# Weight splits behind a norm's vector steps, the mean square and the attention weights on ScalarE

## The chip, the cores and the metric

The kernel runs on one core of a Trainium2 chip. The metric is the device time of one execution in microseconds (us); three runs of the kernel before give 1181.78, 1181.87 and 1183.03, with a median of 1181.87. The engines are called PE (TensorE matmul; PEld is its weight load), ACT (ScalarE), DVE (VectorE), POOL (GpSimd) and SP (SyncE, which only issues DMAs here).

## The reference

Two layers of one block and one of another follow each other on 256 tokens of width 1024, all in fp32:

```python
for l in range(2):                                   # first block, twice
    z = rms_norm(x, g_pre_mix[l]) @ w_in[l]
    q, k, v, cb, cc, cx, ga, gb = split(z)           # 16 heads, 4 kv heads of 64
    y_attn = band_attention(rope(q), rope(k), v, sink) @ w_attn_proj[l]
    y_conv = (cb * short_conv(cc * cx, conv_w[l])) @ w_conv_proj[l]
    mix = (sigmoid(ga) * y_attn + sigmoid(gb) * y_conv) @ w_out[l]
    x = x + rms_norm(mix, g_post_mix[l])
    h = rms_norm(x, g_pre_ffn[l])
    f = (silu(h @ w_gate[l]) * (h @ w_up[l])) @ w_down[l]
    x = x + rms_norm(f, g_post_ffn[l])
mod = silu(c) @ w_cond_2 + b_cond_2                  # second block, once
# shift, scale and gate for each half come from mod; stick-breaking attention and
# a pooling mixer, w_out_2, then the same FFN shape, each with pre and post norm
```

rms_norm multiplies a row by (mean of its squares + 1e-6) to the power -1/2 and by a gain; the attention's p is exp(s - m), divided by the sum of its row plus exp(sink - m).

## The kernel before

The two halves of the tokens are t=0 and t=1, each 128 rows with its x in a tile of 128x1024. All weights are packed on the host into 211 chunks of 128x2048 (1 MB), which are consumed in one order, ORDER. To keep fp32 accuracy on PE every weight and every activation is split into a high part H (a cast to fp32r on ACT, L271) and a low part L (the difference, a DVE subtract, L272), and each product is three matmuls: high by H, low by H, high by L. A chunk is split in two halves of 128x1024; there are nine half buffers for H and nine for L (NSPLIT). get() hands out the next chunk: it issues raw loads on SP's queue up to five chunks ahead (LOOK_RAW, four raw buffers) and splits up to three chunks ahead (LOOK). Chunks of the kind "cond" are used raw, by DVE, and their sum over partitions is made on POOL (L504).

A scheduler sets the order within each engine from its own model of priorities and readiness; hp() gives the vector steps of a norm a higher priority. The names in the rows: mix_out does the wo products (tiles wo), ffn does gate, up and down (pgA/puA, pg/pu, dn; f is the gated product and fHL its two parts). At the end of wo and of dn the last chunks are held (three for wo, TAIL = 4 for dn) and used first for t=0 and then for t=1, so that the norm of t=0 runs while PE works on t=1. That norm is: Post.half (Square of the product with its sum, jk_a..., on ACT, L337; times the gain on DVE, ag, L397), Post.fin (rstd on POOL, L341, L343, L345; x update on DVE, L404, for both halves of the columns), Norm.vec (Square of x, jk_x..., L337; times the gain, xg, L362; rstd; the scale, L366, or L368 where a shift is added), and then Norm.tr: PE transposes (pt, L377) and the copies to the parts of the next input (xf, xm; ACT L207 and DVE L208). There are five such places: after wo and after dn of layer 0, after wo and after dn of layer 1, and after the second block's wo.

The attention of a layer is eight units, one for each of four kv heads and each t, interleaved with the matmuls of the convolution branch (pcc, pcx, pcb). In a unit: qs (split of q), pq (transposes), S (scores), mask and maximum on DVE, exp on ACT (L636, four of 128x256), the sink's exp es, den and its reciprocal rd on DVE (L641), P times rd, four POOL instructions (L643), eight PE transposes PTp (L651), their copies PT on ACT, and po.

Of the kernel before, what the change touches and what calls it, by code (L numbers as in the profile page):

```python
# [10 lines left out]
F32 = mybir.dt.float32  # L11
F32R = mybir.dt.float32r
# [6 lines left out]
P = 128  # L19
# [9 lines left out]
NDOWN = DFF // 256  # L29
TAIL = 4  # L30
EPS = 1e-6
# [127 lines left out]
def tile_model(ctx: ExitStack, tc: tile.TileContext, x_in, wpack, sink, convw, gains, c_in,  # L159
# [84 lines left out]

    state = dict(raw=0, spl=0, use=0)
    raws, HL = {}, {}
# [10 lines left out]

    def emit_split():
        i = state["spl"]
        while state["raw"] <= i:  # L260
            emit_raw()
        if ORDER[i][0] == "cond":
            HL[i] = raws[i]
        else:
            r = raws[i]
            hv = []
            for hf in range(2):
                H = wp.tile([P, CH // 2], F32R, tag="H", name=f"H{i}_{hf}", bufs=NSPLIT)
                L = wp.tile([P, CH // 2], F32R, tag="L", name=f"L{i}_{hf}", bufs=NSPLIT)
                rv = r[:, hf * (CH // 2):(hf + 1) * (CH // 2)]  # L270
                nc.scalar.copy(H, rv)  # L271
                nc.vector.tensor_sub(L, rv, H.bitcast(F32))  # L272
                hv.append((H, L))
            HL[i] = hv
        state["spl"] += 1

    def get(key):
        i = state["use"]
        assert ORDER[i] == key, (ORDER[i], key)
        n = len(ORDER)  # L280
        while state["raw"] < min(i + LOOK_RAW, n):
            emit_raw()
        while state["spl"] < min(i + LOOK, n):
            emit_split()
        state["use"] += 1
        return HL.pop(i)
# [20 lines left out]
    nhalf = cst.tile([P, 1], F32, tag="nhalf", name="nhalf")  # L307
    nc.vector.memset(nhalf, -0.5)
    ident_r = cst.tile([P, P], F32R, tag="identr", name="ident_r")
    nc.vector.tensor_copy(ident_r, ident)  # L310
# [23 lines left out]

    def sumsq(src, c, ssq, name):
        junk = s2(f"jk_{name}{c}")
        nc.scalar.activation(junk, src, AF.Square, accum_out=ssq[:, c:c + 1])  # L337

    def rstd(ssq, name):
        ms = small("ms_" + name, 1)  # L340
        nc.gpsimd.tensor_scalar(ms, ssq[:, 0:1], 1.0 / D, EPS, ALU.mult, ALU.add)  # L341
        m2 = small("m2_" + name, 1)
        nc.gpsimd.tensor_scalar(m2, ssq[:, 1:2], 1.0 / D, ms[:, 0:1], ALU.mult, ALU.add)  # L343
        rs = small("rs_" + name, 1)
        nc.gpsimd.tensor_tensor(rs, m2, nhalf, ALU.pow)  # L345
        return rs

    class Norm:
# [6 lines left out]
        def vec(self):  # L355
            t, name = self.t, self.name
            with hp():
                ssq = small("sx_" + name, 2)
                xg = s4("xg_" + name)
                for c in range(2):  # L360
                    sumsq(xt[t][:, HC[c]], c, ssq, "x" + name)
                    nc.vector.tensor_mul(xg[:, HC[c]], xt[t][:, HC[c]], self.G[:, HC[c]])  # L362
                rs = rstd(ssq, "x" + name)
                for c in range(2):
                    if self.S is None:
                        nc.vector.tensor_scalar(xg[:, HC[c]], xg[:, HC[c]], rs[:, 0:1], None, ALU.mult)  # L366
                    else:
                        nc.vector.scalar_tensor_tensor(xg[:, HC[c]], xg[:, HC[c]], rs[:, 0:1], self.S[:, HC[c]],  # L368
                                                       ALU.mult, ALU.add)
            self.h = xg  # L370
# [101 lines left out]
    def mix_out(l, kts, mp, make_post, after, lead):  # L472
        accs = [[ps1(f"wo{l}_{t}{c}") for c in range(2)] for t in range(2)]
        for i, j in enumerate(kts[:lead]):
            w = get(("wo", l, j))
            tick()
            for t in range(2):
                for c in range(2):
                    mmD2(accs[t], w, mp.ks(0, 2 * j, 2), mp.ks(1, 2 * j, 2), t, c, i == 0, False)
        drain()  # L480
        ch = [(get(("wo", l, j)), mp.ks(0, 2 * j, 2), mp.ks(1, 2 * j, 2)) for j in kts[lead:]]
        row_out(ch, accs, lead > 0, make_post, after)
# [24 lines left out]
    def ffn(l, xp, norms, make_post, after):  # L507
# [28 lines left out]
        for key in order:  # L536
# [13 lines left out]
            else:  # L550
# [9 lines left out]
                else:  # L560
                    tail.append((get(key), fs[j][0], fs[j][1]))
        if l == DEPTH - 1:
# [5 lines left out]
    def attention(l, q, kf, v, op):  # L568
# [35 lines left out]
        def unit(g, t):  # L604
# [37 lines left out]
            for hh in range(4):  # L642
                nc.gpsimd.tensor_scalar(Pt[:, hh, :], Pt[:, hh, :], rd[:, hh:hh + 1], 0.0, ALU.mult, ALU.add)  # L643
            yield SM_DELAY
# [232 lines left out]
    for l in range(DEPTH):  # L877
# [72 lines left out]
    def after3(t, post):  # L950
        post.fin()
        norms[t].vec()
        spawn(norms[t].gen, TR_DELAY)

# [5 lines left out]
    drain()  # L960
    aw = [(get(("wo", 2, j)), mp.ks(0, 2 * j, 2), mp.ks(1, 2 * j, 2)) for j in (0, 1)]
    for t in range(2):
# [74 lines left out]
```

## Time and profile before

| | |
|---|---|
| runs, median | 1181.87 us (1181.78 to 1183.03) |
| profiled execution | 1181.56 us, span 1179.7 us |
| granted PE clock, mean | 0.948 |
| busy PE / PEld / DVE / ACT / POOL | 97% / 81% / 71% / 56% / 11% of the span |
| HBM read | 233.28 MB |

The span is from the first to the last instruction; the execution's own time has 1.9 us more. A row of the timeline gives start, duration, engine, line, operation, output<-inputs, and in brackets how long the engine had been idle and what released it. The wait list gives engine, instruction, what it waited for, then the total in us, the number and the longest. Rows of groups give busy us and the mean in ns; those of windows give for each engine busy us, then the granted clock, the DMA share and GB/s.

### The profile page before, as it was taken

To read this page: it belongs to the slowest core of one execution; us is meant where nothing else is said; L and a number is where in the kernel's file an instruction comes from. 1 tells how busy PE (TensorE), PEld (TensorE's weight loads), DVE (VectorE), ACT (ScalarE), POOL (GpSimd) and SP (SyncE) were. 2 spreads that over 40 slices of the span, in tenths; PEclk is the share of its full clock that TensorE was granted. 3 is DMA by queue.
4 is the path that set the end of the run, shared out by engine and by line. 5 is a ranking of instruction groups with operands and counts; after the bars stand their busy time and mean duration, and the time that the engine had idled before them with its cause. 6 is when DMAs were issued, how large, how long until landed. Compare 5 with 4: busy or idle time off the path is not lost.

```text
span 1179.7 us, 15598 instructions
## 1 busy us (share of the span) xinstructions
PE 1145.0 (97%) x5896; PEld 957.7 (81%) x5896; DVE 837.0 (71%) x1146; ACT 659.6 (56%) x1107; POOL 126.5 (11%) x146
## 2 busy tenths in 40 slices
PE   6999999999999999999999999999999999999997
PEld 4887888878888887887888878888887777888886
DVE  6787845769788757787757768887968448765652
ACT  5775756556555446676646455555455546655451
POOL 0011310010202001013230012020212002000000
PEclk9998999999999999999999999999999999999999
DMA  8742334756666665634447556675865345655520
GB/s 316 281 143 108 136 140 171 268 183 251 240 257 248 223 241 188 241 107 143 144 168 296 198 181 232 233 297 187 314 255 196 127 161 179 245 178 184 201 85 36
DMA packets 36243, 235.36 MB, mean 200 GB/s; under 512 B 4668, under 2 KB 5180, under 8 KB 9416
## 3 DMA queue, kind: packets, MB, share of 16 engines
q1 hardware_dynamic: 33696, 225.41, 52.7%
q10 hardware_dynamic: 2472, 8.96, 2.3%
q8 instruction: 46, 0.75, 0.3%
q14 instruction: 29, 0.24, 0.1%
HBM read 233.28 MB, written 1.07 MB: 199 GB/s over the span
## 4 chain that ended last, share of the span: by engine, by line
PE 49%; DVE 3%; POOL 2%; ACT 2%; issue 1%; POOLq 0%; DVEq 0%; ACTq 0%
PE dn L242 9%; PE pu L242 9%; PE pg L242 8%; PE wo L242 2%; PE pcp L242 2%; PE pap L242 2%; PE pgb L242 2%; PE pga L242 2%; PE puA L242 1%; PE pgA L242 1%; PE pcx L242 1%; PE z L242 1%; PE pv L242 1%; PE p2k L242 1%; PE po L242 1%
## 5 line engine op out<-in xcount | busy, mean ns | idle before, releaser
L272 DVE TENSOR_TENSOR L<-raw,H 128x1024 fp32r<-128x1024 f32 x374 | 476.7, 1284 | 178.2 <-ACT H L271 168.4
L271 ACT CAST H<-raw 128x1024 fp32r<-128x1024 f32 x374 | 390.5, 1050 | 210.3 <-issue 33.8
L242 PE MATMUL dn<-H,fHL 128*128 128x512 f32 x432 | 116.4, 391 | 0.4 <-DVE fHL L548 0.2
L242 PE MATMUL pu<-xf,H 128*128 128x512 f32 x432 | 108.2, 392 | 0.0
L242 PE MATMUL pg<-xf,H 128*128 128x512 f32 x432 | 107.8, 391 | 0.0
L242 PEld LDWEIGHTS dn<-H,fHL 128*128 128x128 f32 x432 | 79.8, 188 | 16.7 <-ACT fHL L547 0.6
L242 PEld LDWEIGHTS pg<-xf,H 128*128 128x128 f32 x432 | 79.2, 188 | 15.2
L242 PEld LDWEIGHTS pu<-xf,H 128*128 128x128 f32 x432 | 77.7, 189 | 13.9
L643 POOL TENSOR_SCALAR P<-P,rd 128x256 f32<-128x256 f32 x64 | 46.9, 750 | 228.2 <-ACT cc L428 107.6
L242 PE MATMUL dn<-L,fHL 128*128 128x512 f32 x216 | 67.1, 390 | 0.0
L242 PEld LDWEIGHTS pg<-xf,L 128*128 128x128 f32 x432 | 58.9, 190 | 4.2
L242 PEld LDWEIGHTS pu<-xf,L 128*128 128x128 f32 x432 | 58.9, 190 | 4.2
L504 POOL PARTITION_ALL_REDUCE mrow<-cacc x6 | 38.9, 6486 | 217.4 <-DMA raw<-in_wpack_dram 177.4
L501 DVE SCALAR_TENSOR_TENSOR cacc<-raw,silu_c,cacc 128x1024 f32<-128x1024 f32 x48 | 61.3, 1277 | 0.2
L242 PE MATMUL pu<-xf,L 128*128 128x256 f32 x432 | 60.2, 282 | 0.0
L242 PE MATMUL pg<-xf,L 128*128 128x256 f32 x432 | 60.2, 282 | 0.0
L242 PE MATMUL wo<-H,m 128*128 128x512 f32 x192 | 52.5, 394 | 0.0
L547 ACT CAST fHL<-f 128x512 fp32r<-128x512 f32 x27 | 16.7, 620 | 57.3 <-DVE f L545 57.3
L242 PEld LDWEIGHTS dn<-L,fHL 128*128 128x128 f32 x216 | 40.6, 188 | 8.5
L242 PEld LDWEIGHTS wo<-H,m 128*128 128x128 f32 x192 | 35.6, 188 | 7.2 <-issue 0.2
L636 ACT ACTIVATE P<-S,nm 128x256 f32<-128x256 f32 x64 | 29.4, 473 | 12.2 <-DVE nm L630 12.2
L541 ACT ACTIVATE s<-s 128x512 f32<-128x512 f32 x27 | 17.1, 632 | 33.1 <-DVE s L429 33.1
(277 smaller groups left out, 2006.4 us busy)
## 6 DMA issues: line engine op xcount, KB each, us to landing
raw<-in_wpack_dram SPq DMA_DIRECT2D x209, 1024.0 KB, 4.9
raw<-in_wpack_dram SPq DMA_DIRECT2D x4, 512.0 KB, 8.8
gpm<-in_gains_dram ACTq DMA_DIRECT2D x3, 512.0 KB, 7.4
gpf<-in_gains_dram ACTq DMA_DIRECT2D x3, 512.0 KB, 8.0
gqf<-in_gains_dram ACTq DMA_DIRECT2D x2, 512.0 KB
out_dram<-x SPq DMA_DIRECT2D x4, 256.0 KB, 2.1
pmat<-in_pmat_dram SPq DMA_DIRECT2D x2, 384.0 KB, 5.5
x<-in_x_dram SPq DMA_DIRECT2D x2, 256.0 KB, 2.6
```

Of the source, the lines that this page charges most:

```text
L242: nc.tensor.matmul(o, a, b, start=start, stop=stop, **kw)
L271: nc.scalar.copy(H, rv)
L272: nc.vector.tensor_sub(L, rv, H.bitcast(F32))
L501: nc.vector.scalar_tensor_tensor(a3, w[:, k], silu_c[:, 2 * j + k:2 * j + k + 1], a3, ALU.mult, ALU.add)
L504: nc.gpsimd.partition_all_reduce(mrow, a, P, bass_isa.ReduceOp.add)
L541: last = nc.scalar.activation(s, s, AF.Silu)
L547: nc.scalar.copy(fHL[:, 0], fv)
L636: nc.scalar.activation(Pt[:, hh, :], S[hh // 2][:, hh % 2, :], AF.Exp, bias=nm[:, hh:hh + 1], accum_out=den[:, hh:hh + 1])
L643: nc.gpsimd.tensor_scalar(Pt[:, hh, :], Pt[:, hh, :], rd[:, hh:hh + 1], 0.0, ALU.mult, ALU.add)
```

## The change

Four things are edited.

- The splits are emitted by halves, and from the end of the first such norm on each split is issued behind the last ACT step (its Identity) and the last DVE step (its scale) of the last t=0 norm. Where chunks are held, no more than nine halves are handed out ahead (cap). TAIL goes from 4 to 3.
- The mean square: the Square has a scale of D to the power -1/2, so that its sum is the mean; an ACT Identity on 128x1 adds eps and, for the second half, the first half's sum. Two POOL steps (L341, L343) go; the power stays on POOL.
- P times rd is an ACT copy with a scale for each partition instead of a POOL instruction: 64 in all.
- A constant tile for eps.

POOL has 112 instructions fewer (64 and 48), ACT 112 more; PE has the same ones.

```diff
--- before.py
+++ after.py
@@ -27,7 +27,7 @@
 DFF = 2816
 NFB = (DFF - 512) // 256
 NDOWN = DFF // 256
-TAIL = 4
+TAIL = 3
 EPS = 1e-6
 NEG = -1e30
 CH = 2048
@@ -242,7 +242,7 @@
         nc.tensor.matmul(o, a, b, start=start, stop=stop, **kw)
 
 
-    state = dict(raw=0, spl=0, use=0)
+    state = dict(raw=0, spl=0, use=0, behind=None)
     raws, HL = {}, {}
 
     def emit_raw():
@@ -255,33 +255,39 @@
         raws[i] = t
         state["raw"] += 1
 
-    def emit_split():
-        i = state["spl"]
+    def behind(e):
+
+        return tc.issue_after(state["behind"][e].ins) if state["behind"] else nullcontext()
+
+    def emit_half():
+        i, hf = divmod(state["spl"], 2)
         while state["raw"] <= i:
             emit_raw()
         if ORDER[i][0] == "cond":
             HL[i] = raws[i]
         else:
-            r = raws[i]
-            hv = []
-            for hf in range(2):
-                H = wp.tile([P, CH // 2], F32R, tag="H", name=f"H{i}_{hf}", bufs=NSPLIT)
-                L = wp.tile([P, CH // 2], F32R, tag="L", name=f"L{i}_{hf}", bufs=NSPLIT)
-                rv = r[:, hf * (CH // 2):(hf + 1) * (CH // 2)]
+            H = wp.tile([P, CH // 2], F32R, tag="H", name=f"H{i}_{hf}", bufs=NSPLIT)
+            L = wp.tile([P, CH // 2], F32R, tag="L", name=f"L{i}_{hf}", bufs=NSPLIT)
+            rv = raws[i][:, hf * (CH // 2):(hf + 1) * (CH // 2)]
+            with behind(0):
                 nc.scalar.copy(H, rv)
+            with behind(1):
                 nc.vector.tensor_sub(L, rv, H.bitcast(F32))
-                hv.append((H, L))
-            HL[i] = hv
+            HL.setdefault(i, []).append((H, L))
         state["spl"] += 1
 
-    def get(key):
+    def get(key, cap=None):
+
         i = state["use"]
         assert ORDER[i] == key, (ORDER[i], key)
         n = len(ORDER)
         while state["raw"] < min(i + LOOK_RAW, n):
             emit_raw()
-        while state["spl"] < min(i + LOOK, n):
-            emit_split()
+        ahead = min(i + LOOK, n) * 2
+        if cap is not None:
+            ahead = max(min(ahead, cap), 2 * i + 2)
+        while state["spl"] < ahead:
+            emit_half()
         state["use"] += 1
         return HL.pop(i)
 
@@ -306,6 +312,8 @@
     nc.sync.dma_start(xt[1], x_in[P:2 * P, :])
     nhalf = cst.tile([P, 1], F32, tag="nhalf", name="nhalf")
     nc.vector.memset(nhalf, -0.5)
+    eps = cst.tile([P, 1], F32, tag="eps", name="eps")
+    nc.vector.memset(eps, EPS)
     ident_r = cst.tile([P, P], F32R, tag="identr", name="ident_r")
     nc.vector.tensor_copy(ident_r, ident)
     modd = dr.tile([6, D], F32, tag="modd", name="modd")
@@ -333,16 +341,15 @@
 
 
     def sumsq(src, c, ssq, name):
+
         junk = s2(f"jk_{name}{c}")
-        nc.scalar.activation(junk, src, AF.Square, accum_out=ssq[:, c:c + 1])
+        nc.scalar.activation(junk, src, AF.Square, scale=D ** -0.5, accum_out=ssq[:, c:c + 1])
+        return nc.scalar.activation(ssq[:, c:c + 1], ssq[:, c:c + 1], AF.Identity,
+                                    bias=eps if c == 0 else ssq[:, 0:1])
 
     def rstd(ssq, name):
-        ms = small("ms_" + name, 1)
-        nc.gpsimd.tensor_scalar(ms, ssq[:, 0:1], 1.0 / D, EPS, ALU.mult, ALU.add)
-        m2 = small("m2_" + name, 1)
-        nc.gpsimd.tensor_scalar(m2, ssq[:, 1:2], 1.0 / D, ms[:, 0:1], ALU.mult, ALU.add)
         rs = small("rs_" + name, 1)
-        nc.gpsimd.tensor_tensor(rs, m2, nhalf, ALU.pow)
+        nc.gpsimd.tensor_tensor(rs, ssq[:, 1:2], nhalf, ALU.pow)
         return rs
 
     class Norm:
@@ -358,14 +365,14 @@
                 ssq = small("sx_" + name, 2)
                 xg = s4("xg_" + name)
                 for c in range(2):
-                    sumsq(xt[t][:, HC[c]], c, ssq, "x" + name)
+                    self.sq = sumsq(xt[t][:, HC[c]], c, ssq, "x" + name)
                     nc.vector.tensor_mul(xg[:, HC[c]], xt[t][:, HC[c]], self.G[:, HC[c]])
                 rs = rstd(ssq, "x" + name)
                 for c in range(2):
                     if self.S is None:
-                        nc.vector.tensor_scalar(xg[:, HC[c]], xg[:, HC[c]], rs[:, 0:1], None, ALU.mult)
+                        self.sc = nc.vector.tensor_scalar(xg[:, HC[c]], xg[:, HC[c]], rs[:, 0:1], None, ALU.mult)
                     else:
-                        nc.vector.scalar_tensor_tensor(xg[:, HC[c]], xg[:, HC[c]], rs[:, 0:1], self.S[:, HC[c]],
+                        self.sc = nc.vector.scalar_tensor_tensor(xg[:, HC[c]], xg[:, HC[c]], rs[:, 0:1], self.S[:, HC[c]],
                                                        ALU.mult, ALU.add)
             self.h = xg
 
@@ -478,7 +485,8 @@
                 for c in range(2):
                     mmD2(accs[t], w, mp.ks(0, 2 * j, 2), mp.ks(1, 2 * j, 2), t, c, i == 0, False)
         drain()
-        ch = [(get(("wo", l, j)), mp.ks(0, 2 * j, 2), mp.ks(1, 2 * j, 2)) for j in kts[lead:]]
+        cap = 2 * state["use"] + NSPLIT
+        ch = [(get(("wo", l, j), cap), mp.ks(0, 2 * j, 2), mp.ks(1, 2 * j, 2)) for j in kts[lead:]]
         row_out(ch, accs, lead > 0, make_post, after)
 
     cacc = [None]
@@ -558,7 +566,8 @@
                         for c in range(2):
                             mmD2(accs[t], w, fs[j][0], fs[j][1], t, c, j == 0, False)
                 else:
-                    tail.append((get(key), fs[j][0], fs[j][1]))
+                    cap = 2 * (state["use"] - len(tail)) + NSPLIT
+                    tail.append((get(key, cap), fs[j][0], fs[j][1]))
         if l == DEPTH - 1:
             with tc.issue_after(last.ins):
                 nc.scalar.preload_act_table_set("natural_log_exp_and_others")
@@ -640,7 +649,7 @@
             rd = small(f"rd{l}{g}{t}", 4)
             nc.vector.reciprocal(rd, den)
             for hh in range(4):
-                nc.gpsimd.tensor_scalar(Pt[:, hh, :], Pt[:, hh, :], rd[:, hh:hh + 1], 0.0, ALU.mult, ALU.add)
+                nc.scalar.activation(Pt[:, hh, :], Pt[:, hh, :], AF.Copy, scale=rd[:, hh:hh + 1])
             yield SM_DELAY
             if t == 0:
                 PT[g] = [s4(f"PT{l}{g}{pr}", (P, 2, 2, T)) for pr in range(2)]
@@ -883,6 +892,8 @@
         def after(t, post):
             post.fin()
             norms[t].vec()
+            if t == 0:
+                state["behind"] = (norms[t].sq, norms[t].sc)
             spawn(norms[t].gen, TR_DELAY)
 
         mix_out(l, [0, 1, 2, 3], mp, lambda t, acc: Post(t, acc, gpm, f"pm{l}{t}"), after, LEAD)
@@ -913,6 +924,8 @@
         def after2(t, post):
             post.fin()
             nn[t].vec()
+            if t == 0:
+                state["behind"] = (nn[t].sq, nn[t].sc)
             spawn(nn[t].gen, TR_DELAY)
 
         ffn(l, xp, norms, mkpost, after2)
@@ -950,6 +963,8 @@
     def after3(t, post):
         post.fin()
         norms[t].vec()
+        if t == 0:
+            state["behind"] = (norms[t].sq, norms[t].sc)
         spawn(norms[t].gen, TR_DELAY)
 
     accs = [[ps1(f"wo2_{t}{c}") for c in range(2)] for t in range(2)]
@@ -958,7 +973,8 @@
         for c in range(2):
             mmD2(accs[t], *pw[i], t, c, i == 0, False)
     drain()
-    aw = [(get(("wo", 2, j)), mp.ks(0, 2 * j, 2), mp.ks(1, 2 * j, 2)) for j in (0, 1)]
+    cap = 2 * (state["use"] - 2) + NSPLIT
+    aw = [(get(("wo", 2, j), cap), mp.ks(0, 2 * j, 2), mp.ks(1, 2 * j, 2)) for j in (0, 1)]
     for t in range(2):
         post = Post(t, accs[t], Pm, f"pm2{t}")
         left = pw[max(0, WO2_LEAD - 2):] if t == 1 else []
```

The rows that follow are each engine's order of instructions; numbers behind a name are those of its buffer, and "x4" four alike in a row.

PE in the third attention unit of layer 0 (where PTp starts 97 us in), before and then after. P is the attention's weight tile, pcc a product of the convolution branch, pq and S belong to the next unit:

```order
L242 MATMUL pcc_0_969<-x_124,L_0_797 128x256 x2
L242 MATMUL pcc_0_969<-x_132,L_0_797 128x256 x2
L242 MATMUL pcc_0_969<-x_135,L_0_797 128x256 x2
L651 MATMUL PTp_1012<-ident,P_910 128x128 x4
L651 MATMUL PTp_1018<-ident,P_910 128x128 x4
L242 MATMUL pcc_1_1024<-x_121,H_1_800 128x512 x2
L242 MATMUL pcc_1_1024<-x_124,H_1_800 128x512 x2
L242 MATMUL S_1029<-kTh_423,qT_998 128x256
```

```order
L242 MATMUL pcc_0_967<-x_124,L_0_795 128x256 x2
L242 MATMUL pcc_0_967<-x_132,L_0_795 128x256 x2
L242 MATMUL pcc_0_967<-x_135,L_0_795 128x256 x2
L660 MATMUL PTp_1010<-ident,P_908 128x128 x4
L660 MATMUL PTp_1016<-ident,P_908 128x128
L242 MATMUL pcc_1_1022<-x_121,H_1_798 128x512 x2
L660 MATMUL PTp_1016<-ident,P_908 128x128 x3
L242 MATMUL pcc_1_1022<-x_124,H_1_798 128x512 x2
L242 MATMUL S_1027<-kTh_421,qT_996 128x256
```

Two pcc matmuls now stand between the fifth and the sixth transpose.

ACT in the same unit, before and after:

```order
L636 ACTIVATE P_910,den_909<-S_890,nm_905 128x256 x2
L636 ACTIVATE P_910,den_909<-S_891,nm_905 128x256 x2
L638 ACTIVATE es_907<-es_907 128x4
L207 CAST y_955<-yc_853 128x2x256
L207 CAST o_986<-po_977 128x2x256
L271 CAST H_1_1152<-raw_959 128x1024
L616 CAST qT_998<-pq_993 128x512
L428 COPY cc_958<-pcc_0_969 128x256
L607 CAST qs_1098<-q_154 128x4x64
L653 COPY PT_1010<-PTp_1012 128x4x128
L653 COPY PT_1011<-PTp_1018 128x4x128
```

```order
L645 ACTIVATE P_908,den_907<-S_888,nm_903 128x256 x2
L645 ACTIVATE P_908,den_907<-S_889,nm_903 128x256 x2
L647 ACTIVATE es_905<-es_905 128x4
L207 CAST y_953<-yc_851 128x2x256
L207 CAST o_984<-po_975 128x2x256
L625 CAST qT_996<-pq_991 128x512
L652 ACTIVATE P_908<-P_908,rd_915 128x256 x4
L435 COPY cc_956<-pcc_0_967 128x256
L662 COPY PT_1008<-PTp_1010 128x4x128
L662 COPY PT_1009<-PTp_1016 128x4x128
L616 CAST qs_1096<-q_152 128x4x64
L273 CAST H_1_1150<-raw_957 128x1024
```

The four scales of P stand behind the cast of qT, and the casts H of the weights and the copy of qs behind the copies of PT.

DVE after wo of layer 0, from the gain of t=0's second half on, before and after (raw, H and L are weights; ag and xg are the products with the gains, x_72 is t=0's x, x_73 t=1's):

```order
L397 TENSOR_TENSOR ag_pm_2357<-wo_01_2262,gpm_2257 128x512
L404 SCALAR_TENSOR_TENSOR x_72<-ag_pm_2357,rs_apm_2386,x_72 128x512
L272 TENSOR_TENSOR L_1_2335<-raw_2308,H_1_2334 128x1024
L362 TENSOR_TENSOR xg_nf_2391<-x_72,gpf_2259 128x512
L404 SCALAR_TENSOR_TENSOR x_72<-ag_pm_2357,rs_apm_2386,x_72 128x512
L272 TENSOR_TENSOR L_0_2499<-raw_2318,H_0_2498 128x1024
L362 TENSOR_TENSOR xg_nf_2391<-x_72,gpf_2259 128x512
L366 TENSOR_SCALAR xg_nf_2391<-xg_nf_2391,rs_xnf_2402 128x512 x2
L397 TENSOR_TENSOR ag_pm_2425<-wo_10_2263,gpm_2257 128x512
L272 TENSOR_TENSOR L_1_2503<-raw_2318,H_1_2502 128x1024
L208 TENSOR_TENSOR xf_2446<-pt_nf_2441,xf_2446 128x2x128
L272 TENSOR_TENSOR L_0_2509<-raw_2328,H_0_2508 128x1024
```

```order
L404 TENSOR_TENSOR ag_pm_2351<-wo_01_2260,gpm_2255 128x512
L411 SCALAR_TENSOR_TENSOR x_72<-ag_pm_2351,rs_apm_2378,x_72 128x512 x2
L369 TENSOR_TENSOR xg_nf_2383<-x_72,gpf_2257 128x512 x2
L373 TENSOR_SCALAR xg_nf_2383<-xg_nf_2383,rs_xnf_2392 128x512 x2
L275 TENSOR_TENSOR L_1_2485<-raw_2306,H_1_2484 128x1024
L404 TENSOR_TENSOR ag_pm_2415<-wo_10_2261,gpm_2255 128x512
L275 TENSOR_TENSOR L_0_2489<-raw_2316,H_0_2488 128x1024
L275 TENSOR_TENSOR L_1_2493<-raw_2316,H_1_2492 128x1024
L208 TENSOR_TENSOR xf_2437<-pt_nf_2432,xf_2437 128x2x128
L275 TENSOR_TENSOR L_0_2499<-raw_2326,H_0_2498 128x1024
L404 TENSOR_TENSOR ag_pm_2415<-wo_11_2262,gpm_2255 128x512
L208 TENSOR_TENSOR xf_2440<-pt_nf_2432,xf_2440 128x2x128
```

The two updates of x, the two products and the two scales now stand together; three L's that stood among them or beside them come behind.

ACT after dn of layer 1, before and after (scl_m and sh_m are the second block's scale and shift, loaded by DMAs of ACT's queue; g2pre is its gain):

```order
L294 DMA gqf_7884<-in_gains_dram 128x1024
L505 DMA modd<-mrow_7850 1x1024
L337 ACTIVATE jk_apf_7919,sa_pf_7917<-dn_00_6828 128x512
L294 DMA g2pre<-in_gains_dram 128x1024
L902 DMA scl_m<-modd 128x1024
L905 DMA sh_m<-modd 128x1024
L337 ACTIVATE jk_apf_7946,sa_pf_7917<-dn_01_6829 128x512
L271 CAST H_1_7869<-raw_7838 128x1024
```

```order
L300 DMA gqf_7878<-in_gains_dram 128x1024
L513 DMA modd<-mrow_7848 1x1024
L273 CAST H_1_7867<-raw_7836 128x1024
L273 CAST H_0_7873<-raw_7851 128x1024
L300 DMA g2pre<-in_gains_dram 128x1024
L346 ACTIVATE jk_apf_7907,sa_pf_7905<-dn_00_6802 128x512
L913 DMA scl_m<-modd 128x1024
L347 ACTIVATE sa_pf_7905<-sa_pf_7905,eps 128x1
L916 DMA sh_m<-modd 128x1024
```

Two casts H stand ahead of the first Square, and scl_m's DMA still behind it; the Square is of a product that PE now makes two groups later.

## The prediction

> **What bounds the kernel now.** I read the busy lines first, then the list of waits for TensorE (PE), then the timeline at the places that the waits name.
>
> ```profile
> PE 1145.0 (97%) x5896; PEld 957.7 (81%) x5896; DVE 837.0 (71%) x1146; ACT 659.6 (56%) x1107; POOL 126.5 (11%) x146
> PE pt_n L377 <- DVE xg_n L366: 9.4, 1, 9.4
> PE PTp L651 <- POOL P L643: 5.9, 6, 1.2
> PE pt_nf L377 <- DVE xg_nf L366: 3.4, 4, 1.3
> PE pt_nm L377 <- DVE xg_nm L368: 1.5, 2, 1.1
> PE pt_nm L377 <- DVE xg_nm L366: 1.4, 1, 1.4
> PE pt_nf L377 <- DVE xg_nf L368: 1.3, 1, 1.3
> PE ptf L516 <- DVE sA L531: 1.3, 1, 1.3
> PE p2q L242 <- DVE xm L208: 0.8, 1, 0.8
> PE dn L242 <- DVE fHL L548: 0.2, 1, 0.2
> ```
>
> PE is busy for 97% of the span, and the change leaves its work alone, so all that can be won is PE's waiting. Apart from the start (9.4 us before the first transpose) it is in two kinds of place. One is the attention, where the transposes PTp wait for POOL to scale P; the other is the norm boundaries (pt, xm, fHL), where the transposes of the normed rows wait for VectorE's last step. One unit of the attention (started 96 us in) looks like this:
>
> ```profile
> 96.33 0.61 ACT L616 CAST qT<-pq 128x512 fp32r<-128x512 f32 x1
> 96.39 0.17 DVE L641 RECIPROCAL rd<-den 128x4 f32<-128x4 f32 x1
> 96.72 3.01 POOL L643 TENSOR_SCALAR P<-P,rd 128x256 f32<-128x256 f32 x4 [8.33 <-DVE rd L641]
> 97.05 1.22 DVE L272 TENSOR_TENSOR L<-raw,H 128x1024 fp32r<-128x1024 f32 x1
> 97.25 0.14 PEld L651 LDWEIGHTS PTp<-ident,P 128*128 128x128 f32 x1 [0.91 <-POOL P L643]
> 98.67 0.31 PEld L651 LDWEIGHTS PTp<-ident,P 128*128 128x128 f32 x3 [1.28 <-POOL P L643]
> 99.33 0.14 PEld L651 LDWEIGHTS PTp<-ident,P 128*128 128x128 f32 x1 [0.35 <-POOL P L643]
> 99.79 0.35 PEld L651 LDWEIGHTS PTp<-ident,P 128*128 128x128 f32 x3 [0.31 <-POOL P L643]
> 100.19 2.06 PE L242 MATMUL pcc<-x,H 128*128 128x512 f32 x4
> 100.20:102.50 2.30, 2.30 (x9) 1.92 (x8) 0.00 (x0) 0.58 (x1) 0.00 (x0) 0.50 0.92 388
> PEld PTp L651 <- POOL P L643: 9.7, 14, 1.4
> ```
>
> PE's weight loads stop four times, 0.91 + 1.28 + 0.35 + 0.31 = 2.85 us, and after it the granted clock is 0.50 for 2.3 us: four matmuls take 2.06 us. The loads' total, 9.7 us in 14 stops, is the attention's full stall over both layers; the matmuls' 5.9 us leaves out the part hidden in the pipeline.
>
> **P scaled on ACT.** It removes 64 POOL instructions and adds 64 to ACT. The rows for the price:
>
> ```profile
> L643 POOL TENSOR_SCALAR P<-P,rd 128x256 f32<-128x256 f32 x64 | 46.9, 750 | 228.2 <-ACT cc L428 107.6
> L636 ACT ACTIVATE P<-S,nm 128x256 f32<-128x256 f32 x64 | 29.4, 473 | 12.2 <-DVE nm L630 12.2
> L859 ACT ACTIVATE m<-ppl,pscale x4: 473/474/476, 958.6 to 964.1; 128x256 fp32r<-128x256 f32 x4
> 65.00:162.00 97.00, 93.58 (x571) 79.14 (x570) 75.91 (x162) 65.56 (x156) 23.46 (x32) 0.93 0.35 123
> ```
>
> ACT's exp of the same shape takes 473 ns and a copy with a per-partition scale 474, so four cost about 1.9 us against POOL's mean of 4 x 0.750 = 3.0. In the unit above the four POOL instructions took 3.01 us because L ran on VectorE for 1.22 us beside them. [...]
>
> In that unit rd is done at 96.56, the cast of qT, behind which the scales now stand, at 96.94, and four scales end at about 96.94 + 1.9 = 98.85; the last two transposes follow by about 99.1. The next matmul started at 100.19. PE's new order also puts two pcc matmuls (2 x 0.23 at full clock) in the middle of the transposes. I take 1.1 + 0.45 = 1.6 us of the 2.85. The other two stopping units of a layer hold the rest: 9.7 / 2 - 2.85 = 2.0 us a layer; there POOL's stretching goes too, and I take 1.7. Two layers: 2 x (1.6 + 1.7) = 6.6. The half clock after the long stop cost about four matmuls x 0.23 = 0.9 us in layer 0, and I take it back as a gain too, since the stop becomes shorter. Against it stands VectorE's new order: in the second unit of each layer one more L (1.22 us) stands between es and the reciprocal rd, which eats the 0.6 us by which P was early there, 0.5 us lost per layer. Sum for attention: -6.6 - 0.9 + 1.0 = -6.5 us. Bounds: nothing, if ACT stands behind other work as long as POOL was stretched; -10.6 (9.7 + 0.9), if all stops go. I am nearer to the full one since ACT's duration is known from two rows.
>
> The price on ACT is 32 x 0.473 = 15 us in each attention stage. ACT is busy 65.6 of 97 us there, so 81 of 97 with it: it becomes fuller than VectorE (75.9). What is queued behind: the copies of PT and of the PSUM tiles, and the weights' casts H. ACT is in order, so while it waits for rd nothing behind runs; between es and P stand only the casts of y, o and qT. The cover is the look-ahead: the wait list has no stop of PE on H or L there. [...]
>
> **Splits behind the norm, and the mean square.** The boundary after wo of layer 0:
>
> ```profile
> 255.67 0.75 DVE L404 SCALAR_TENSOR_TENSOR x<-ag_pm,rs_apm,x 128x512 f32<-128x512 f32 x1 [0.38 <-POOL rs_apm L345]
> 256.34 1.22 DVE L272 TENSOR_TENSOR L<-raw,H 128x1024 fp32r<-128x1024 f32 x1
> 258.08 0.74 DVE L404 SCALAR_TENSOR_TENSOR x<-ag_pm,rs_apm,x 128x512 f32<-128x512 f32 x1
> 258.97 0.63 ACT L337 ACTIVATE jk_xnf<-x 128x512 f32<-128x512 f32 x1
> 259.88 0.82 POOL L343 TENSOR_SCALAR m_xnf<-sx_nf,ms_xnf 128x1 f32<-128x1 f32 x1 [2.27 <-ACT jk_xnf L337]
> 260.77 0.55 POOL L345 TENSOR_TENSOR rs_xnf<-m_xnf,nhalf 128x1 f32<-128x1 f32 x1
> 261.36 0.88 DVE L366 TENSOR_SCALAR xg_nf<-xg_nf,rs_xnf 128x512 f32<-128x512 f32 x2 [0.81 <-POOL rs_xnf L345]
> 261.91 0.66 PE L377 MATMUL pt_nf<-ident,xg_nf 128*128 128x128 f32 x4 [1.27 <-DVE xg_nf L366]
> 262.16 0.68 DVE L397 TENSOR_TENSOR ag_pm<-wo,gpm 128x512 f32<-128x512 f32 x1
> 264.15 1.18 PE L242 MATMUL pgA<-H,xf 128*128 128x512 f32 x4
> 272.11 0.66 PE L377 MATMUL pt_nf<-ident,xg_nf 128*128 128x128 f32 x4 [0.38 <-DVE xg_nf L366]
> L638 ACT ACTIVATE es<-es x16: 211/214/223, 72.8 to 588.2; 128x4 f32<-128x4 f32 x16
> ```
>
> The second update of x waits 1.66 us (256.42 to 258.08) behind an L and a product; POOL's m_xnf takes 0.82 us beside an L. After the change no L stands there, so the second Square starts at about 257.3 instead of 258.97, and its mean takes an ACT Identity on 128x1. No row has that; between nothing and the 0.214 us of the small exp, I take 0.21. The scale then comes at 257.3 + 0.8 + 0.2 + 0.2 + 0.6 = 259.1 instead of 261.36, and PE, there at 261.91 - 1.27 = 260.64, finds it done: -1.27. But the halves that VectorE had done inside the chain now come behind the scale. In the order stand L, ag, L, L ahead of the first low part of xf: 3 x 1.22 + 0.68 = 4.3 us from 259.9, which ends at 264.2, while PE needed xf 2.24 us after the first transposes (261.91 to 264.15), now near 263.0: a new wait of about 1 us. At t=1 the smaller stop (0.38) is half gone. Net -0.9 from the whole walk to the third puA group; bounds -1.65 (both stops go, nothing new) to +0.6 (a new wait twice as long as I take). Layer 1 has the same shape: -0.9.
>
> Behind the FFN of layer 0, TAIL 3 gives the same order as after wo: -1.3 and +0.7, -0.6. Behind the FFN of layer 1, the fHL stop (0.2 + 0.2 in the list) goes, but a DMA moves:
>
> ```profile
> 869.69 0.60 ACT L337 ACTIVATE jk_apf<-dn 128x512 f32<-128x512 f32 x1 [2.23 <-PE dn L242]
> 870.09 0.44 ACTq L902 DMA_DIRECT2D scl_m<-modd  x1
> 875.93 1.22 DVE L903 SCALAR_TENSOR_TENSOR g2pre<-scl_m,g2pre 128x1024 f32<-128x1024 f32 x1 [4.00 <-DMA scl_m<-modd]
> ```
>
> ACT's queue issues scl_m behind the first Square jk_apf, and TAIL 3 lets that Square start two groups later (about 2.7 us), so scl_m lands at about 878.5; VectorE multiplies g2pre ahead of the update of x. The chain after it would then end about where it did, less the L's that stood in it: -0.4, bounds -2.4 (pt_nm, xm and fHL stops go) and +2.7 (the whole delay arrives). Behind wo2 the stop of 1.3 goes, but transposes are placed a group earlier and the L's follow: 0, bounds -1.3 and +1. The sA stop (1.3) sits after POOL's all-reduce and is not touched: 0, bounds -0.5 and +1. The start loses two POOL steps and gets two Identities: -0.3 with the end's. The longer ACT queue at the norms (48 x 0.21 us in all) is covered by ACT's idle 44%. The 48 POOL instructions go from POOL's queue, on which nothing else waits. One raw load moves behind the pmat loads in SP's queue; the raws are five chunks ahead.
>
> **Sum.** -6.5 - 0.9 - 0.9 - 0.6 - 0.4 + 0 + 0 - 0.3 = -9.6 us, from the profiled execution's 1181.56 (its span of 1179.7 and 1.9 around it) to 1172.0. The median of the runs is 0.3 above that execution, inside what runs differ by, so I keep 1172.0. About 0.2%, 2.4 us, can be told from no change.
>
> **Rivals.** (1) *ACT's queue eats the gain in attention.* In-order ACT stands at the first scale until rd comes, then H, cc and PT run late, and PE waits for these. For: ACT goes to 84% there, rd itself hangs on L's that wait for H on ACT. Against: no wait of PE on H or L now. Attention then gives 0 and the boundaries -3: 1178.5, or 1181 if these give little. (2) *Full gain*: all attention stops (-10.6) and the pt stops without new xf waits (3.4 + 1.5 + 1.4 from the list, and the 0.8 of xm): 1181.6 - 10.6 - 7.1 = 1164. Against: the L's have to run sometime, and PE needs their weights right after. (3) *Slower*: the scales delay ACT so much that the splits run late for PE in each unit. A unit's scales hold the H behind them by 1.9 us; if the halves in hand are worth less than this, PE waits the rest in each of 16 units. It decides from 0.8 us a unit on, 16 x 0.8 = 13 against the 9.6: 1185; at 1.2 us, 1191. (4) *The boundaries turn*: new waits on xf and on scl_m are worth +1 each instead of -0.6: attention's gain alone with +4: 1179.
>
> **Chances.** The forecast (1168 to 1176) 0.55; rival 1 0.15 (half of it within 0.2%); rival 2 0.08; rival 3 0.10; rival 4 0.12 (mostly still faster). To hold 8 in 10, the range runs from 1165 to 1180: it leaves out rival 3, half of rival 2 and the dearer half of rival 1. The forecast's own range is 1168 to 1176. Faster 0.77, same 0.13, slower 0.10.
>
> **What would show it.** Right: PTp has waits of under 3 us in all, now on ACT; the stop after wo names xf and no longer xg; no granted clock of 0.5 near 100 us; ACT's copy of P near 0.47 us. Wrong: PE's list names H, L, cc or PT in the attention; or pt_nm waits for g2pre by more than 2 us; or the xf waits pass 1.5 us a boundary.

## The result and the profile after

The changed kernel takes 1169.01 us (median of 4 runs, 1167.79 to 1169.62) against 1181.82 beside it: a ratio of 0.9892, interval 0.988 to 0.9903, or 12.8 us. 1172.0 was forecast, with a range of 1165 to 1180. The profiled execution took 1169.62, its span 1167.8 us.

Busy time and the waits of PE and of its weight loads (PEld) that the change touches, after (engine, instruction, what it waited for, total us, times, longest):

```profile
PE 1143.3 (98%) x5896; PEld 956.9 (82%) x5896; DVE 829.6 (71%) x1147; ACT 694.6 (59%) x1219; POOL 56.2 (5%) x34
PE pgA L242 <- DVE xf L208: 2.3, 3, 1.0
PE PTp L660 <- ACT P L652: 1.1, 4, 0.3
PEld PTp L660 <- ACT P L652: 3.7, 12, 0.5
PE pt_nm L384 <- DVE xg_nm L375: 1.1, 2, 0.9
PE pq L242 <- DVE xm L208: 0.9, 1, 0.9
PE pt_nf L384 <- DVE xg_nf L375: 0.6, 1, 0.6
PE S L242 <- ACT qT L625: 0.4, 2, 0.2
PE p2q L242 <- DVE xm L208: 0.4, 1, 0.4
```

PE's work is the same; PTp's wait fell from 5.9 to 1.1 us (that of its weight loads from 9.7 to 3.7), and behind wo the wait for the transposes (xg) has become one for xf. Where the time went is read from when PE starts the same matmul in both timelines. The differences (after minus before, us; minus is earlier), with what was forecast for the stretch:

| stretch of PE's timeline | measured | forecast |
|---|---|---|
| start, to the first scores S | +0.4 | -0.3 with the end |
| attention of layer 0 (S to the transposes ahead of wo) | -3.9 | -6.5 for both layers |
| attention of layer 1 | -2.5 | |
| wo of layer 0 to the first gate chunk | -1.1 | -0.9 |
| dn of layer 0 to the next layer's kv | -0.6 | -0.6 |
| wo of layer 1, to the end of the first up chunks (puA) | -0.9 | -0.9 |
| the sA stop behind it | -1.3 | 0 |
| dn of layer 1 to the second block's keys | -1.6 | -0.4 |
| the second block's mixer | -0.5 | 0 |
| its wo | +0.2 | 0 |

Their sum is -11.8, what PE's last matmul shows (1173.11 to 1161.26). (sA is the gated product of the first chunks, which PE transposes in ptf.) The two profiled executions are 11.9 us apart (1181.56 and 1169.62), the medians of the runs 12.8.

The attention unit of the prediction, in the timeline after:

```profile
96.23 0.17 DVE L650 RECIPROCAL rd<-den 128x4 f32<-128x4 f32 x1
96.50 1.71 ACT L652 ACTIVATE P<-P,rd 128x256 f32<-128x256 f32 x4
97.07 1.12 PE L660 MATMUL PTp<-ident,P 128*128 128x128 f32 x5 [0.22 <-ACT P L652]
97.95 0.71 PE L242 MATMUL pcc<-x,H 128*128 128x512 f32 x2
98.49 0.49 PE L660 MATMUL PTp<-ident,P 128*128 128x128 f32 x3
100.20:102.50 2.30, 2.30 (x16) 2.08 (x15) 2.30 (x6) 1.80 (x3) 0.00 (x0) 1.00 0.00 0
L652 ACT ACTIVATE P<-P,rd 128x256 f32<-128x256 f32 x64 | 27.4, 504 | 0.9 <-DVE rd L650 0.7
65.00:162.00 97.00, 96.07 (x597) 80.22 (x596) 74.98 (x163) 78.39 (x189) 0.00 (x0) 1.00 0.37 132
```

Four scales take 1.71 us where POOL took 3.01, PE does two pcc matmuls in the gap, and the stretch that had a clock of 0.50 has 1.00. ACT is not the faster engine for it: POOL's scale had a median of 0.481 us in the kernel before, ACT's has 0.495, with 0.543 at most. What goes is the stretching on POOL, where single scales took up to 2.50 us and the mean was 0.750. ACT is busy for 78.4 of the 97 us.

The boundary after wo of layer 0:

```profile
252.05 1.41 DVE L411 SCALAR_TENSOR_TENSOR x<-ag_pm,rs_apm,x 128x512 f32<-128x512 f32 x2 [0.26 <-POOL rs_apm L352]
254.13 0.28 ACT L347 ACTIVATE sx_nf<-sx_nf,eps 128x1 f32<-128x1 f32 x1
254.44 0.30 ACT L347 ACTIVATE sx_nf<-sx_nf 128x1 f32<-128x1 f32 x1
254.82 0.55 POOL L352 TENSOR_TENSOR rs_xnf<-sx_nf,nhalf 128x1 f32<-128x1 f32 x1 [2.80 <-ACT sx_nf L347]
255.40 0.88 DVE L373 TENSOR_SCALAR xg_nf<-xg_nf,rs_xnf 128x512 f32<-128x512 f32 x2 [0.73 <-POOL rs_xnf L352]
256.20 1.22 DVE L275 TENSOR_TENSOR L<-raw,H 128x1024 fp32r<-128x1024 f32 x1
256.98 0.60 PE L384 MATMUL pt_nf<-ident,xg_nf 128*128 128x128 f32 x4
257.93 2.35 DVE L275 TENSOR_TENSOR L<-raw,H 128x1024 fp32r<-128x1024 f32 x2
260.20 0.41 DVE L208 TENSOR_TENSOR xf<-pt_nf,xf 128x256 fp32r<-128x256 f32 x1
260.67 0.95 PE L242 MATMUL pgA<-H,xf 128*128 128x512 f32 x3 [0.80 <-DVE xf L208]
```

From the first update of x to the scale it takes 3.35 us (252.05 to 255.40) where it took 5.69 (255.67 to 261.36). PE finds the transposes' input done, and 3.7 us later stops 0.8 us for xf, which stands behind three L's.

### The profile page after: what moved, and what is told of

Same layout as the page of the kernel before. It is cut to its first block, busy times and chain, and to the rows that moved or that the text cites. A ratio compares the mean times of both kernels' runs of the same rounds, so it can differ in the third digit from the quotient of the medians.

```text
span 1167.8 us, 15484 instructions
## 1 busy us (share of the span) xinstructions
PE 1143.3 (98%) x5896; PEld 956.9 (82%) x5896; DVE 829.6 (71%) x1147; ACT 694.6 (59%) x1219; POOL 56.2 (5%) x34
## 4 chain that ended last, share of the span: by engine, by line
PE 90%; ACT 4%; DVE 3%; issue 1%; DMA 1%; POOL 1%; SPq 0%; DVEq 0%; POOLq 0%; ACTq 0%
PE dn L242 14%; PE pu L242 14%; PE pg L242 13%; PE pq L242 4%; PE pcx L242 4%; PE pcp L242 4%; PE wo L242 4%; PE pap L242 4%; PE pga L242 4%; PE pgb L242 4%; PE pcb L242 3%; PE pgA L242 2%; PE puA L242 2%; PE pcc L242 2%; PE pkv L242 2%; PE po L242 2%
## 5 line engine op out<-in xcount | busy, mean ns | idle before, releaser
L275 DVE TENSOR_TENSOR L<-raw,H 128x1024 fp32r<-128x1024 f32 x374 | 471.6, 1272 | 182.0 <-ACT H L273 172.9
L242 PE MATMUL pcp<-H,y 128*128 128x512 f32 x128 | 35.4, 396 | 0.0
L242 PE MATMUL pap<-H,o 128*128 128x512 f32 x128 | 35.2, 394 | 0.0
```

The lines of the kernel that those rows point to most:

```text
L242: nc.tensor.matmul(o, a, b, start=start, stop=stop, **kw)
```

## The experiments

Ratios are to the kernel before, run beside each.

**P on ACT alone.**

```diff
-                nc.gpsimd.tensor_scalar(Pt[:, hh, :], Pt[:, hh, :], rd[:, hh:hh + 1], 0.0, ALU.mult, ALU.add)
+                nc.scalar.activation(Pt[:, hh, :], Pt[:, hh, :], AF.Copy, scale=rd[:, hh:hh + 1])
```

> The kernel before with P scaled on ACT, nothing else. Theory A (each part pays in its own place): the two attention stages lose together 6 to 6.5 us (about 4 in layer 0, where the half clock after the long stop goes too, 2.5 in layer 1), every boundary stays as before; 1175.3. Theory B (the parts need each other: without POOL free of the norms' small steps, or with the L's still in the norm's chain, ACT's queue gives the gain back): under 3 us, 1179 or more. Theory C (the gain is the granted clock, 0.948 before and 0.999 after, not the stops): this run is as fast as its clock says, whatever its stops are.

Measured: 1175.07, 6.9 us less (0.9944, 0.9928 to 0.9961). The attention stages gave 4.0 and 2.5 us in the timeline. That is theory A; theory B falls for this part.

**The changed kernel with P on POOL** (the same lines, the other way).

> The changed kernel with P scaled on POOL again. Theory A: the attention's stops of the kernel before return (two layers, about 4.7 us of late starts each), boundaries as in the changed kernel; 1175 to 1176. Theory B: more than half of the gain goes, 1177 or more. Theory C: the time follows the clock that is granted in this run.

Measured: 1177.63, 4.4 us less (0.9965, 0.9952 to 0.9978); the rest of the change without P. 6.9 and 4.4 make 11.3 of the 12.8. By its number this is theory B's (1177 or more), 1.6 us above theory A's: putting P back cost 8.6 us where P alone had gained 6.9. By the timeline it is theory A's (its profiled execution, 1175.87, is the fastest of five): the boundaries kept their gain, and the attention of layer 1 lost 1.0 us against the kernel before, where the half clock now fell too:

```profile
533.00:535.00 2.00, 2.00 (x8) 1.38 (x7) 0.00 (x0) 0.89 (x2) 0.65 (x2) 0.50 0.94 250
```

In the profile before it was in layer 0 alone; here and with the next two kernels it was also in layer 1, behind the same stop, and with the short stops of P on ACT alone and of the changed kernel it was in neither layer. The other executions of the kernel before have mean clocks from 0.994 to 0.998, so it seems to come and go there too; one such stretch, 3.4 us at half, takes 0.0014 off the mean. Layer 1's gain was therefore read from an execution without it.

**The mean square alone**, in the kernel before (rows L341 and L343 of POOL out, Square scaled, two Identities in).

> The kernel before with the mean square on ACT alone (splits, TAIL and P as before). Theory A: POOL's two stretched steps (0.8 to 2.5 us each beside an L) go from the chains, but the L's remain in them and an Identity of 0.29 us comes in: 0 to 1.5 us faster, 1180.3 to 1181.8. Rival: the mean square is the main part of the boundaries' gain (5 us), 1177; then the splits matter little.

Measured: 1180.81, 1.2 us less, not clear of no change (0.9994, 0.9984 to 1.0003), in theory A's range. The stops for the transposes fell only from 1.3 to 0.8 and 0.9 us behind wo, and rose to 2.7 behind dn of layer 1.

**The splits alone**: the changed kernel with P and the mean square on POOL.

> The changed kernel with P and the mean square on POOL again: the halves, the queueing behind the norm, the cap and TAIL 3 remain. Theory A: the boundaries keep most of their gain of 4 to 5 us, since no L stands in the chain and POOL's steps are then not stretched: 1177 to 1178, and PE's wait for xf in place of that for the transposes. Rival (the mean square carries it): 1180 or more.

Measured: 1183.87, 1.9 us more (1.0018, 1.0009 to 1.0027). The rival's number (1180 or more) holds, but its reason does not, since the mean square alone carries only 1.2: the two edits that I had put into one term cost 1.9 and gave 1.2 alone, and give 4.4 together. This run and the one before also settle theory C: their granted clock is 0.996 and they are as slow as the kernel before, whose profile had 0.948 and whose other executions had up to 0.998.

**TAIL 4** in the changed kernel.

> The changed kernel with TAIL 4 (eight of nine half buffers held behind dn). Theory A: only the two places behind dn change. There the kernel with TAIL 3 gained 0.6 and 1.6 us; TAIL 4 brings the fHL stop of 0.8 us back at layer 1 and lets scl_m start 2.7 us earlier, so 0 to 1 us slower, 1169 to 1170. Rival: TAIL carries the gain behind dn, since with it fewer than nine halves are left for the next weights: 2 us slower or more, 1171.

Measured: 1170.35 (0.99, 0.9886 to 0.9915), 1.3 more than the changed kernel in the medians, inside the interval, and between the two expectations. The timelines have 1.3 us too, 0.9 of it behind dn of layer 1, where pt_nm waits 1.6 instead of 0.9 us and fHL 0.4 again. The earlier start of scl_m bought nothing: it was issued at 860.8 instead of 862.9 us, and g2pre started at 867.7 instead of 867.6.

**No queueing behind the norm.**

```diff
-        return tc.issue_after(state["behind"][e].ins) if state["behind"] else nullcontext()
+        return nullcontext()
```

> The changed kernel without the queueing behind the norm's last steps (halves, cap, TAIL 3, mean square and P as changed). Theory A (it is the queueing that keeps the L's out of the chain, and it is worth its price only because POOL's steps are gone): waits for the transposes of 1 us return behind wo and dn, those for xf go down; 2 to 4 us slower, 1171 to 1173. Rival: what the queueing gives at the transposes it takes back at xf, so without it the time is the same within 1 us, 1168 to 1170.

Measured: 1169.4 (0.9891, 0.9876 to 0.9905): the same time. The rival is right. In its list the transposes wait again, 0.8 and 0.9 us behind wo of the two layers (below), and pgA for xf not at all:

```profile
PE pt_nf L384 <- DVE xg_nf L373: 1.7, 2, 0.9
```

**Whole chunks**: P and the mean square on ACT, TAIL 3, and the old splits.

> The kernel before with P on ACT, the mean square on ACT and TAIL 3, but splits by whole chunks, three ahead, not capped and not queued. P alone gave 6.9 us, the mean square alone 1.2, TAIL about 1.3. Theory A (these add up): 1172.5 to 1173.5, and the halves with the cap are worth the other 3 to 4 us of the changed kernel's 13. Rival (the mean square's gain is only set free by TAIL or by P leaving POOL, and halves and cap are worth nothing): 1169 to 1170.

Measured: 1173.55, 9.0 less (0.9927, 0.9912 to 0.9942), the upper end of theory A's range. So halves and cap are worth about 4 us; 2.6 of it is behind dn of layer 1. There the timeline has two L's ahead of steps of t=0's chain and two more beside its power, which takes 1.80 us (0.55 in the kernel before):

```profile
872.42 1.21 DVE L272 TENSOR_TENSOR L<-raw,H 128x1024 fp32r<-128x1024 f32 x1
874.15 0.74 DVE L404 SCALAR_TENSOR_TENSOR x<-ag_pf,rs_apf,x 128x512 f32<-128x512 f32 x1
874.82 1.22 DVE L272 TENSOR_TENSOR L<-raw,H 128x1024 fp32r<-128x1024 f32 x1
876.55 2.35 DVE L272 TENSOR_TENSOR L<-raw,H 128x1024 fp32r<-128x1024 f32 x2
877.52 1.80 POOL L345 TENSOR_TENSOR rs_xnm<-sx_nm,nhalf 128x1 f32<-128x1 f32 x1 [6.40 <-ACT sx_nm L340]
880.25 0.96 PE L377 MATMUL pt_nm<-ident,xg_nm 128*128 128x128 f32 x5 [3.00 <-DVE xg_nm L368]
881.80:885.20 3.40, 3.40 (x10) 2.73 (x9) 3.40 (x8) 2.14 (x7) 0.00 (x0) 0.50 0.62 248
```

A half clock follows this stop of 3.00 us as well (last row). Nine matmuls take 3.57 us there, 881.98 to 885.55, against 2.04 at the pace ahead of the stop (six in 1.36), so in this execution about 1.5 of the 2.6 us are the clock's.

**Halves and cap with the mean square on POOL**, not queued (the splits-alone kernel with the edit above).

> The kernel before with halves, cap and TAIL 3, P and the mean square on POOL, and no queueing behind the norm. With the queueing this was 1183.87, 1.9 over the kernel before. Theory A (the queueing did the harm: L's put behind t=0's scale ran beside t=1's small POOL steps and stretched one to 2.5 us, where PE then stopped 0.6 to 2.0 us for the second transposes): without it the halves keep part of their 4.5 us, 1178 to 1181. Rival (halves and cap give nothing while POOL's two steps are in the chain, wherever the L's stand): 1182 to 1184.

Measured: 1182.13 (1.0005, 0.9994 to 1.0015): nothing gained, the rival's 1182. The queueing may have done part of the harm (1.9 us with it, 0.5 without, the intervals overlap). The gain is taken at t=1, where PE stops at all five boundaries for the second transposes, 0.6 to 1.1 us each; the first one, behind wo of layer 0:

```profile
268.49 2.53 POOL L348 TENSOR_SCALAR ms_xnf<-sx_nf 128x1 f32<-128x1 f32 x1 [2.01 <-ACT jk_xnf L344]
268.50 0.75 DVE L411 SCALAR_TENSOR_TENSOR x<-ag_pm,rs_apm,x 128x512 f32<-128x512 f32 x1
269.16 1.22 DVE L275 TENSOR_TENSOR L<-raw,H 128x1024 fp32r<-128x1024 f32 x1
270.29 0.69 DVE L369 TENSOR_TENSOR xg_nf<-x,gpf 128x512 f32<-128x512 f32 x1
272.60 0.66 PE L384 MATMUL pt_nf<-ident,xg_nf 128*128 128x128 f32 x4 [0.63 <-DVE xg_nf L373]
```

POOL's first small step takes 2.53 us beside an x update, an L and a product in a row: it ends at 271.02, 0.04 us after the product (270.98), and PE stops 0.63 us for t=1's transposes.

**P shared by ACT and POOL.**

```diff
-                nc.scalar.activation(Pt[:, hh, :], Pt[:, hh, :], AF.Copy, scale=rd[:, hh:hh + 1])
+                if hh % 2 == 0:
+                    nc.scalar.activation(Pt[:, hh, :], Pt[:, hh, :], AF.Copy, scale=rd[:, hh:hh + 1])
+                else:
+                    nc.gpsimd.tensor_scalar(Pt[:, hh, :], Pt[:, hh, :], rd[:, hh:hh + 1], 0.0, ALU.mult, ALU.add)
```

> The changed kernel with P's first and third head scaled on ACT, second and fourth on POOL. Theory A (PTp waits for the time that four scales take in a row): the first two heads are done in one step and all four in two, so of the 3.9 us of late starts that are left in the attention 1.5 to 3 go: 1166 to 1167.5. Rival (POOL's half is stretched by L's beside it, up to 1.5 us, and comes last): same or up to 3 us slower, 1169 to 1172.

Measured: 1164.66 (0.9858, 0.9844 to 0.9873), 4.4 us below the changed kernel, more than theory A's 1166 to 1167.5. The same unit:

```profile
94.76 1.21 POOL L655 TENSOR_SCALAR P<-P,rd 128x256 f32<-128x256 f32 x2 [8.79 <-DVE rd L650]
95.62 0.90 ACT L653 ACTIVATE P<-P,rd 128x256 f32<-128x256 f32 x2
96.17 1.09 PE L663 MATMUL PTp<-ident,P 128*128 128x128 f32 x8 [0.24 <-ACT P L653]
```

The eight transposes run in one piece. POOL's half was ready at 95.97, although its two took 1.21 us. The waits of PTp's weight loads fall from 3.7 to 1.4 us over both layers, and the attention as a whole by 4.6 in the timeline; the rest of that was not taken apart.

**The shared P without queueing.**

> P shared by ACT and POOL, and no queueing behind the norm. Theory A (the two places are apart, and the queueing only moves the wait from the transposes to xf): as with P shared alone, 1164 to 1165.5. Rival (the shared P needs POOL, and L's that stand in the norm's chain make POOL late): 1166 or more.

Measured: 1164.28 (0.985, 0.9833 to 0.9866): the same as the shared P, as theory A had it.

**P on VectorE.**

> The changed kernel with P scaled on VectorE (DVE). Its scale of 128x512 with a per-partition operand takes 0.48 us (the norm's), so one of 128x256 should take about 0.27, four 1.1 us against 1.9 on ACT, and they start right behind rd on the same engine. Theory A (the length of the four in a row sets PTp's wait): the late starts of 3.9 us fall to under 2: 1166.5 to 1168. Rival (DVE, busy 74 of 90 us there, is the fuller engine, and what stands behind P, the L's and the masks, comes late): 1170 to 1173.

Measured: 1170.03 (0.9898, 0.9884 to 0.9913), the lower edge of the rival's range. One scale takes 0.347 us, not 0.27, and the stops at PTp go down to two; one of 2.0 us comes in, since VectorE gets to the low part of qs late:

```profile
L652 DVE TENSOR_SCALAR P<-P,rd x64: 335/347/355, 74.3 to 581.7; 128x256 f32<-128x256 f32 x64
PE pq L622 <- DVE qs L617: 2.0, 1, 2.0
```

Against the changed kernel the attention of layer 0 gained 2.0 us and that of layer 1, where this stop falls, lost 1.7; a half clock follows the stop (0.50 from 571.2 to 574.5 us).

**L's behind the first low part of xf** instead of behind the scale (state["behind"] is set again by Norm.tr, to the first subtract of put).

> The changed kernel with the L's queued behind the first low part of xf (of t=0) instead of behind the scale. Theory A (the three L's and the product ahead of it make the new wait of 1 us at each of three boundaries): these waits go, 2 to 3 us faster, 1166 to 1167. Rival (the weights are then late): PE waits for L instead, by as much or more: 1169 to 1173.

Measured: 1172.56 (0.9919, 0.9903 to 0.9936), 3.5 us more than the changed kernel; the number is in the rival's range. The waits for xf fell as hoped (2.3 to 1.3 us), but the L's now fall together with POOL's sum over partitions at layer 1:

```profile
PE ptf L529 <- DVE sA L544: 3.3, 1, 3.3
PE pgA L245 <- DVE xf L208: 1.3, 3, 0.8
712.00 7.83 DVE L278 TENSOR_TENSOR L<-raw,H 128x1024 fp32r<-128x1024 f32 x3
712.28 6.93 POOL L517 PARTITION_ALL_REDUCE mrow<-cacc  x1 [15.26 <-DVE cacc L514]
720.10:723.40 3.30, 2.92 (x9) 2.53 (x10) 3.30 (x5) 0.59 (x1) 0.00 (x0) 0.50 0.79 251
```

Three L's take 7.83 us, where three in a row took 3.48 in the kernel before (at 877.67), and sA stands behind them. PE waits here neither for xf nor for weights, but for what VectorE had still to do: a place that neither theory named. The stop of 3.3 us is again followed by a half clock (last row).

## Why the prediction was right, and where it was wrong

In the timeline the change gave 2.2 us more than forecast. The sA stop (1.3) and dn of layer 1 (1.2) are the bulk of it; that the other differences nearly cancel is luck.

**P on ACT: right in the sum.** -6.5 was forecast; the timelines gave 6.4, the kernel with this edit alone 6.9 in its median. The mechanism was as told: shorter stops (9.7 to 3.7 us of PTp's weight loads), and no half clock behind them (1.00 where it was 0.50). Inside it two terms were off. The loss of 0.5 us a layer in the second unit, from the L ahead of rd, did not come: no stop stands there. In its place PE waits for S behind the cast of qT, 0.2 us twice (ACT's queue, rival 1 in small), and each layer has a new short stop in its fifth unit. A scale took 0.504 us as a mean, not 0.473, but four in a row end after 1.71, less than 4 x 0.504 = 2.02, since they overlap.

**Splits and mean square: the sum right in part by luck, the reason wrong.** The walk from wo had both edits in one chain, and its -0.9 met -1.1 and -0.9; the new stop at xf, forecast as 1 us, was 0.8 and 1.0. But the walk's own terms (-1.27, +1 and half of -0.38) make about -0.5, not -0.9. In the trace of layer 0 they are -1.27, +0.80 and the whole -0.38, which make -0.85. I also gave the gain to the queueing behind the norm. The runs say otherwise: taking the queueing out changes nothing, halves with the cap are worth nearly 4 us (a half clock saved among them), and only together with the mean square on ACT. Each alone leaves the other wait: L's in the chain of t=0, or POOL's steps stretched beside L's at t=1 (2.53 us for one).

**ACT's Identity** took 0.28 and 0.30 us, outside the bound of 0.214 that I took from the small exp; with two in a row it is 0.6 us where I had 0.2. The scale came at 255.40, which is 258.92 on the old timeline (wo started 3.52 earlier), against 259.1 forecast: the back-to-back Squares made up for it.

**dn of layer 1: forecast -0.4, measured -1.6.** That scl_m starts about two groups later was right:

```profile
862.91 0.36 ACTq L913 DMA_DIRECT2D scl_m<-modd  x1
867.63 1.23 DVE L914 SCALAR_TENSOR_TENSOR g2pre<-scl_m,g2pre 128x1024 f32<-128x1024 f32 x1 [3.32 <-DMA scl_m<-modd]
874.62 0.63 PE L384 MATMUL pt_nm<-ident,xg_nm 128*128 128x128 f32 x4 [0.88 <-DVE xg_nm L375]
```

PE is 9.93 us ahead by then, so 862.91 is 872.84 on the old timeline, 2.75 later than 870.09. But the transfer came after 4.7 us instead of 5.8, and PE's first stop was 0.9 us where it had been 1.1, the second 0.2 where it had been 0.4; with fHL's gone and xm's halved the place gave 1.2 us more than I took. The kernel with TAIL 4 shows why the later start cost little: issued 2.1 us earlier, scl_m brought g2pre no sooner. What sets its landing stays open.

**The sA stop: forecast untouched, gone.** I read it as the price of POOL's sum over partitions alone. It is that sum and what VectorE has queued beside it. Before:

```profile
713.06 6.13 POOL L504 PARTITION_ALL_REDUCE mrow<-cacc  x1 [7.09 <-PE pgA L242]
713.38 6.42 DVE L272 TENSOR_TENSOR L<-raw,H 128x1024 fp32r<-128x1024 f32 x2 [1.05 <-ACT H L271]
726.74 0.66 PE L516 MATMUL ptf<-ident,sA 128*128 128x128 f32 x4 [1.28 <-DVE sA L531]
```

And after:

```profile
703.12 6.13 POOL L512 PARTITION_ALL_REDUCE mrow<-cacc  x1 [6.44 <-DVE cacc L509]
704.75 5.12 DVE L275 TENSOR_TENSOR L<-raw,H 128x1024 fp32r<-128x1024 f32 x2 [0.57 <-ACT H L273]
716.08 0.68 DVE L539 TENSOR_TENSOR sA<-puA,sA 128x512 f32<-128x512 f32 x1
```

PE is 8.6 us ahead here, the sum starts 9.94 us earlier, and two L's lose 1.3 us less to it (5.12 us instead of 6.42). The sum's input, the last cacc, is done 8.5 us earlier, as PE is; what went is most of the time between it and the sum (1.7 us before, 0.2 after). What held the sum there was not tried.

**The start** cost 0.4 instead of gaining 0.3: PE's first transpose did come 0.29 us sooner, but its first matmuls ran at half pace (four of 128x512 in 1.91 us, later in 1.09) until about 19.0 instead of 18.0 us. Over the profiles of all kernels the end of the start lies between 1.2 us earlier and 1.7 later than before, among the variants of the changed kernel alone between 0.7 earlier and 1.7 later, so I take it for chance. The mixer's -0.5 is no gain of the change either: every other profile, the slower kernels' too, shows it against that one of before.

**Rivals.** Rivals 1 and 3 did not come: no wait of PE on H, L, cc or PT, with ACT at 78 of 97 us. Of rival 4 the new wait on xf came, but behind wo it was smaller than the stop that went, and the wait on scl_m did not grow. Rival 2's full gain was out of reach for the changed kernel, since 3.7 us of stops of PTp's weight loads stay in the attention; the shared P took the time to what rival 2 had. The best version is the shared P without queueing, 1164.28 us, not told apart from that with queueing (1164.66).

## What to carry to other kernels

A chain with two waits in it, an L in front of the x update and a POOL step stretched beside the same L's (2.53 us, where the shortest took 0.19), is not paid off edit by edit: neither edit alone made the kernel clearly faster (one cost 1.9 us), both gave 4.4 us. An order that is forced by hand moves the wait to the next thing behind it (from the transposes to xf, from xf to sA), so ask what stands in the queue and not only what is moved; having less in the queue (halves, a cap) did what ordering did not. And where four short instructions in a row gate another engine, look at sharing them: here ACT and POOL with two each (1164.7 us) beat ACT with four (1169.0) and VectorE, the fastest for one of them (0.347 us), with four (1170.0). Other pairs were not tried.

## What the runs showed of the hardware

The column of the granted clock was 0.948 in the one profile before and 0.996 to 1.0 in all others, with the matmuls of 128x512 of gate, up and down at 391 to 393 ns before and after; only a real half clock (0.50) showed in the time. That half clock lasted 3.4 us in the profile before (99.8 to 103.2) and stood over stretches of 3.3 to 3.4 us in three others (above). It came behind the 2.9 us of stops in the attention at one of two like places, or at both, and behind single stops of 2.0, 3.00 and 3.3 us in three other kernels (P on VectorE, whole chunks, L's behind xf). Stops of 2.0 and 2.7 us in two others (splits alone, mean square alone) brought none by the mean clock: it is 0.996 in both profiles, an estimated 0.003 under the changed kernel's 0.999, which is what the two stretches in the attention take off. Where it followed, the place cost about 1.0 to 1.5 us more than its stops (1.0 in layer 1 with P on POOL, 1.5 in whole chunks). What decides behind which of the like stops it comes was not shown. A POOL tensor_scalar on 128x1 took 0.19 us at its shortest in the kernel before, and 2.53 in halves and cap, beside an x update, an L and a product of VectorE in a row.
